# Batch norm over two DMA rings: hand-placed semaphores replaced by the framework's own dependencies

## The chip, the cores and the metric

One Trainium2 chip, one core. The metric is the device time of the slowest (here: the only) core in microseconds (us), lower is better. A kernel is compared with the kernel before in alternating rounds on one chip. A ratio is the mean time of one kernel's fast runs over that of the other's of the same rounds, so it is not quite the ratio of the medians quoted.

## The reference

```python
n, c, h, w = 32, 256, 128, 128          # x is float32, 537 MB; the output is as large
eps = 1e-5
return gamma * (x - mean) / np.sqrt(var + eps) + beta      # one scale and one shift per channel
```

The kernel turns this into `x * scale + shift` with 128 channels on the partitions: 64 tiles of 128 x 16384 float32 (8.389 MB, 64 KB per partition). Each tile is loaded, changed in place, and stored. There are three tile buffers.

## The kernel before

Loads are issued from the SP queue (one DMA ring), stores from the ACT queue (another ring). VectorE does columns 0 to 14336 of a tile in two pieces (the first of STEP = 2560 columns), ACT the rest. Every wait is written by hand inside a critical section.

```python
STEP = 2560; VCOLS = 14336; VLAST = 9216; NBUF = 3
# ... semaphores loaded[s], stored[s], vdone, adone, early, fetched, vec, act (cut)
with tc.tile_critical():
    # ... first half of tile 0, parameters, second half of tile 0 (cut)
    for i in range(1, NT):
        s, turn = i % NBUF, i // NBUF
        if turn:
            nc.sync.wait_ge(stored[s], 16 * turn)                  # store i-3 has left the buffer
        inst = nc.sync.dma_start(out=bufs[s][:], in_=xr[i]).then_inc(loaded[s], 16)
        if turn:
            inst._wait_ge(vdone, 2 * (i - 1) + 1)                  # first piece of tile i-1 is done
    # ... scale and shift (cut)
    vector_part(0, 0, HW // 2)._wait_ge(early, 16)
    vector_part(0, HW // 2, VCOLS)._wait_ge(*landed(0))
    for i in range(1, NT):
        vector_part(i, 0, STEP)._wait_ge(*landed(i))
        vector_part(i, STEP, VLAST if i == last else VCOLS)
    for i in range(last):
        nc.scalar.wait_ge(vdone, 2 * (i + 1))                      # both VectorE pieces of tile i
        inst = scalar_part(i, VCOLS)
        if i:
            inst._wait_ge(stored[(i - 1) % NBUF], 16 * ((i - 1) // NBUF + 1))   # store i-1 landed
        store(i)
    # ... last tile (cut)
```

So each ring is paced: load i+1 is held until load i has landed and its first piece is done; store i until store i-1 has landed and ACT has done its slice of tile i.

Of the kernel before, what the change touches and what calls it, by code (L numbers as in the profile page):

```python
# [8 lines left out]
NBUF = 3  # L9


STEP = 2560
VCOLS = 14336
VLAST = 9216


@with_exitstack
def kernel(
    ctx: ExitStack,
    tc: tile.TileContext,  # L20
    x: bass.AP,
    gamma: bass.AP,
    beta: bass.AP,
    running_mean: bass.AP,
    running_var: bass.AP,
    out: bass.AP,
):
    nc = tc.nc
    eps = 1e-5
    f32 = mybir.dt.float32  # L30

    N, C, H, W = x.shape
    P = nc.NUM_PARTITIONS
    assert C % P == 0
    NCB = C // P
    HW = H * W
    NT = N * NCB
    B = 32
    NQ = P // B
    NE = 16  # L40
    NPAR = 4

    xr = x.rearrange("n (cb p) h w -> (n cb) p (h w)", p=P)
    outr = out.rearrange("n (cb p) h w -> (n cb) p (h w)", p=P)

    params = ctx.enter_context(tc.tile_pool(name="params", bufs=1))
    data = ctx.enter_context(tc.tile_pool(name="data", bufs=1))
    bufs = [data.tile([P, HW], f32, name=f"t{s}", tag=f"t{s}") for s in range(NBUF)]
    rows = params.tile([B, NPAR * C], f32, name="rows", tag="rows")
    turned = params.tile([B, NPAR * C], f32, name="turned", tag="turned")  # L50
    par = params.tile([P, NPAR, NCB], f32, name="par", tag="par")
    eps_t = params.tile([P, 1], f32, name="eps_t", tag="eps")
    std_t = params.tile([P, NCB], f32, name="std_t", tag="std")
    rstd_t = params.tile([P, NCB], f32, name="rstd_t", tag="rstd")
    scale_t = params.tile([P, NCB], f32, name="scale_t", tag="scale")
    ms_t = params.tile([P, NCB], f32, name="ms_t", tag="ms")
    shift_t = params.tile([P, NCB], f32, name="shift_t", tag="shift")



    loaded = [tc.alloc_semaphore(f"loaded{s}") for s in range(NBUF)]
    stored = [tc.alloc_semaphore(f"stored{s}") for s in range(NBUF)]
    early = tc.alloc_semaphore("early")
    vdone = tc.alloc_semaphore("vdone")
    adone = tc.alloc_semaphore("adone")
    fetched = tc.alloc_semaphore("fetched")
    vec = tc.alloc_semaphore("vec")
    act = tc.alloc_semaphore("act")

    with tc.tile_critical():  # L70
        count = [0]

        def step(inst, sem=None, value=None):

            if sem is not None:
                inst._wait_ge(sem, value)
            elif count[0]:
                inst._wait_ge(vec, count[0])
            inst.then_inc(vec, 1)
            count[0] += 1  # L80
            return count[0]

        left, right = slice(0, HW // 2), slice(HW // 2, HW)
        last = NT - 1



        nc.sync.dma_start(out=bufs[0][:, left], in_=xr[0][:, left]).then_inc(early, 16)
        zeroed = step(nc.vector.memset(rows[:], 0.0))  # L89
        for r, ap in enumerate((running_var, gamma, beta, running_mean)):  # L90
            inst = nc.sync.dma_start(out=rows[0:NE, r * C : (r + 1) * C], in_=ap.partition_broadcast(NE))  # L91
            if r == 0:
                inst._wait_ge(vec, zeroed)
            inst.then_inc(fetched, 16)
        nc.sync.dma_start(out=bufs[0][:, right], in_=xr[0][:, right]).then_inc(loaded[0], 16)  # L95
        for i in range(1, NT):
            s, turn = i % NBUF, i // NBUF


            if turn:  # L100
                nc.sync.wait_ge(stored[s], 16 * turn)
            inst = nc.sync.dma_start(out=bufs[s][:], in_=xr[i]).then_inc(loaded[s], 16)
            if turn:
                inst._wait_ge(vdone, 2 * (i - 1) + 1)


        step(nc.vector.memset(eps_t[:], eps))  # L107
        step(nc.vector.transpose(out=turned[:], in_=rows[:]), fetched, 16 * NPAR)  # L108

        blocks = turned.rearrange("p (rc q b) -> p rc q b", q=NQ, b=B)  # L110
        flat = par.rearrange("p r cb -> p (r cb)")
        for q in range(NQ):
            placed = step(nc.vector.tensor_copy(out=flat[q * B : (q + 1) * B], in_=blocks[:, :, q, 0]))  # L113
        var_t, gamma_t, beta_t, mean_t = (par[:, r] for r in range(NPAR))
        nc.scalar.activation(  # L115
            out=std_t[:],
            in_=var_t,
            func=mybir.ActivationFunctionType.Sqrt,
            bias=eps_t[:],
            scale=1.0,  # L120
        )._wait_ge(vec, placed).then_inc(act, 1)
        step(nc.vector.reciprocal(out=rstd_t[:], in_=std_t[:]), act, 1)  # L122
        step(nc.vector.tensor_mul(out=scale_t[:], in0=gamma_t, in1=rstd_t[:]))  # L123
        step(nc.vector.tensor_mul(out=ms_t[:], in0=mean_t, in1=scale_t[:]))  # L124
        ready = step(nc.vector.tensor_sub(out=shift_t[:], in0=beta_t, in1=ms_t[:]))  # L125
        nc.vector.wait_ge(vec, ready)

        def vector_part(i, first, end):
            t, cb = bufs[i % NBUF], i % NCB
            return nc.vector.tensor_scalar(  # L130
                out=t[:, first:end],
                in0=t[:, first:end],
                scalar1=scale_t[:, cb : cb + 1],
                scalar2=shift_t[:, cb : cb + 1],
                op0=mybir.AluOpType.mult,
                op1=mybir.AluOpType.add,
            ).then_inc(vdone, 1)

        def scalar_part(i, first):
            t, cb = bufs[i % NBUF], i % NCB  # L140
            return nc.scalar.activation(  # L141
                out=t[:, first:],
                in_=t[:, first:],
                func=mybir.ActivationFunctionType.Identity,
                bias=shift_t[:, cb : cb + 1],
                scale=scale_t[:, cb : cb + 1],
            ).then_inc(adone, 1)

        def landed(i):
            return loaded[i % NBUF], 16 * (i // NBUF + 1)  # L150

        def store(i):
            s = i % NBUF
            nc.scalar.dma_start(out=outr[i], in_=bufs[s][:])._wait_ge(adone, i + 1).then_inc(stored[s], 16)

        vector_part(0, 0, HW // 2)._wait_ge(early, 16)
        vector_part(0, HW // 2, VCOLS)._wait_ge(*landed(0))
        for i in range(1, NT):
            vector_part(i, 0, STEP)._wait_ge(*landed(i))
            vector_part(i, STEP, VLAST if i == last else VCOLS)  # L160
        for i in range(last):
            nc.scalar.wait_ge(vdone, 2 * (i + 1))
            inst = scalar_part(i, VCOLS)
            if i:
                inst._wait_ge(stored[(i - 1) % NBUF], 16 * ((i - 1) // NBUF + 1))
            store(i)
        scalar_part(last, VLAST)._wait_ge(*landed(last))
        nc.scalar.wait_ge(vdone, 2 * NT)
        store(last)

        for s in range(NBUF):
            nc.sync.wait_ge(stored[s], 16 * ((NT - s + NBUF - 1) // NBUF))


# [28 lines left out]
```

## Time and profile before

| | before |
|---|---|
| median of 3 runs (range) | 2484.66 us (2484.28 to 2487.45) |
| VectorE / ACT busy | 508.8 us / 139.8 us |
| DMA | 9 in all 40 slices, 432 GB/s on the mean |
| period of one tile, both rings | 38.6 us |
| pause of the load ring, landing to next issue | 1.66 us |
| pause of the store ring, landing to next issue | about 2.1 us |

"Busy" is engine time. A DMA slice of 9 means that the 16 DMA engines were moving packets for 90% or more of that fortieth of the span. Issue to landing is the time from the instruction that issues a transfer to the semaphore that reports it complete. The lines behind the table stand in the prediction.

### The profile page before, as it was taken

What the parts mean: (1) busy time and instruction counts of PE and PEld (TensorE: products, weight loads), DVE (VectorE), ACT (ScalarE), POOL (GpSimd) and SP (SyncE); (2) the same over time, 40 slices, a digit from 0 to 9 for tenths busy, and PEclk for the clock granted to TensorE, in tenths of its full rate; (3) what the DMA queues carried; (4) which work ended last, traced back from release to release, by engine and by line L of the source; (5) the groups of instructions that cost most, each with busy time, mean ns of one, the idle gap of its engine ahead of it and who ended that gap; (6) DMA issues with size and microseconds to landing.
All of it is one profiled execution on the core that took longest, in us unless ns stands there. A gap on an engine that the chain in (4) does not pass through costs nothing.

```text
span 2483.3 us, 516 instructions
## 1 busy us (share of the span) xinstructions
DVE 508.8 (20%) x139; ACT 139.8 (6%) x66; POOL 0.2 (0%) x4
## 2 busy tenths in 40 slices
DVE  3122121221212212122121221212212122121220
ACT  0000000000000000000000000000000000000001
POOL 0000000000000000000000000000000000000000
DMA  9999999999999999999999999999999999999999
GB/s 415 430 439 434 428 436 436 435 433 430 432 433 438 430 432 433 435 424 437 437 428 436 438 436 429 437 435 430 436 437 436 430 437 435 429 437 435 433 433 408
DMA packets 18708, 1073.85 MB, mean 432 GB/s; under 512 B 2128, under 2 KB 2192, under 8 KB 2192
## 3 DMA queue, kind: packets, MB, share of 16 engines
q1 hardware_dynamic: 9488, 536.94, 50.1%
q10 hardware_dynamic: 9216, 536.88, 49.9%
q14 instruction: 4, 0.03, 0.0%
HBM read 536.94 MB, written 536.87 MB: 432 GB/s over the span
## 4 chain that ended last, share of the span: by engine, by line
DMA 93%; DVE 4%; another core or an unknown queue 1%; ACT 0%; issue 0%; SPq 0%; DVEq 0%
DMA t<-in_x_dram 93%; DVE t L130 4%; ACT t L141 0%; SPq L91 0%; DVE rows L89 0%; SPq L95 0%; DVE eps_t L107 0%; DVEq L198 0%; SPq L70 0%
## 5 line engine op out<-in xcount | busy, mean ns | idle before, releaser
L130 DVE TENSOR_SCALAR t<-t,scale_t,shift_t 128x11776 f32<-128x11776 f32 (+2 forms) x128 | 505.3, 3989 | 1930.4 <-DMA t<-in_x_dram 1930.2
L141 ACT ACTIVATE t<-t,shift_t,scale_t 128x2048 f32<-128x2048 f32 x64 | 138.2, 2159 | 2299.3 <-DMA out_dram<-t 2276.6
L108 DVE STREAM_TRANSPOSE turned<-rows 32x1024 f32<-32x1024 f32 x1 | 1.2, 1233 | 12.5 <-DMA rows<-in_running_mean_dram 12.5
L115 ACT ACT_TABLE_LOAD x1 | 1.3, 1283 | 0.9 <-SPq L70 0.9
L89 DVE MEMSET rows<- 32x1024 f32 x1 | 0.9, 912 | 1.2 <-SPq L70 1.2
L115 ACT ACTIVATE std_t<-par,eps_t 128x2 f32<-128x2 f32 x1 | 0.3, 296 | 14.7 <-DVE par L113 14.7
L113 DVE COPY par<-turned 32x8 f32<-32x8 f32 x4 | 0.6, 161 | 0.1
L122 DVE RECIPROCAL rstd_t<-std_t 128x2 f32<-128x2 f32 x1 | 0.2, 166 | 0.4 <-ACT std_t L115 0.4
L125 DVE TENSOR_TENSOR shift_t<-par,ms_t 128x2 f32<-128x2 f32 x1 | 0.2, 161 | 0.0
L124 DVE TENSOR_TENSOR ms_t<-par,scale_t 128x2 f32<-128x2 f32 x1 | 0.2, 161 | 0.0
L123 DVE TENSOR_TENSOR scale_t<-par,rstd_t 128x2 f32<-128x2 f32 x1 | 0.2, 160 | 0.0
L187 POOL MEMSET const-bfloat16-1.0<- 128x1 bf16 x1 | 0.1, 101 | 0.0
L187 POOL MEMSET const-uint8-127<- 128x1 uint8 x1 | 0.1, 101 | 0.0
L187 POOL MEMSET const-float32-0.0<- 128x1 f32 x1 | 0.1, 98 | 0.2 <-issue 0.2
L187 POOL MEMSET const-float32-1.0<- 128x1 f32 x1 | 0.1, 98 | 0.0
L107 DVE MEMSET eps_t<- 128x1 f32 x1 | 0.1, 59 | 0.1
## 6 DMA issues: line engine op xcount, KB each, us to landing
t<-in_x_dram SPq DMA_DIRECT2D x2, 4096.0 KB, 16.5
out_dram<-t ACTq DMA_DIRECT2D x64, 36.5
t<-in_x_dram SPq DMA_DIRECT2D x63, 37.0
rows<-in_running_var_dram SPq DMA_DIRECT2D x1, 16.0 KB, 11.3
rows<-in_gamma_dram SPq DMA_DIRECT2D x1, 16.0 KB, 11.1
rows<-in_beta_dram SPq DMA_DIRECT2D x1, 16.0 KB, 10.9
rows<-in_running_mean_dram SPq DMA_DIRECT2D x1, 16.0 KB, 11.3
```

The costliest lines, as they stand in the source:

```text
L89: zeroed = step(nc.vector.memset(rows[:], 0.0))
L107: step(nc.vector.memset(eps_t[:], eps))
L108: step(nc.vector.transpose(out=turned[:], in_=rows[:]), fetched, 16 * NPAR)
L113: placed = step(nc.vector.tensor_copy(out=flat[q * B : (q + 1) * B], in_=blocks[:, :, q, 0]))
L115: nc.scalar.activation(out=std_t[:], in_=var_t, func=mybir.ActivationFunctionType.Sqrt, bias=eps_t[:], scale=1.0,)._wait_ge(vec, placed).t ...
L122: step(nc.vector.reciprocal(out=rstd_t[:], in_=std_t[:]), act, 1)
L123: step(nc.vector.tensor_mul(out=scale_t[:], in0=gamma_t, in1=rstd_t[:]))
L124: step(nc.vector.tensor_mul(out=ms_t[:], in0=mean_t, in1=scale_t[:]))
L125: ready = step(nc.vector.tensor_sub(out=shift_t[:], in0=beta_t, in1=ms_t[:]))
L130: return nc.vector.tensor_scalar(out=t[:, first:end], in0=t[:, first:end], scalar1=scale_t[:, cb : cb + 1], scalar2=shift_t[:, cb : cb + 1 ...
L141: return nc.scalar.activation(out=t[:, first:], in_=t[:, first:], func=mybir.ActivationFunctionType.Identity, bias=shift_t[:, cb : cb + 1] ...
L187: nc = _bacc.Bacc("TRN2", target_bir_lowering=False, num_devices=1)
```

## The change

The intent is to keep the same order and pace of both rings, but let the framework (Tile) derive the waits from the accesses. Only two dependencies, those that pace the rings, are still named. The long diff, cut to its core:

```diff
-    bufs = [data.tile([P, HW], f32, name=f"t{s}", tag=f"t{s}") for s in range(NBUF)]
+    data = ctx.enter_context(tc.tile_pool(name="data", bufs=NBUF))
+    ctx.enter_context(tc.manual_schedule())
+    def after(inst, other):
+        info = mybir.DependencyInfo(mybir.DependencyClass.Sync, mybir.DependencyReason.DATA)
+        tc.add_manual_dep(inst.ins, other.ins.name, info, reason="pace of the rings")
+    def load(i):
+        t = data.tile([P, HW], f32, tag="t")
+        tiles[i] = t
+        return nc.sync.dma_start(out=t[:], in_=xr[i])
-    (twelve semaphores, the critical section, every wait_ge, _wait_ge and then_inc)
-    (three small tiles std_t, rstd_t, ms_t)
+    (one small tile tmp_t in their place)
+    for i in range(NT):
+        if i == 0:
+            vector_part(0, 0, HW // 2)
+            vector_part(0, HW // 2, VCOLS)
+        else:
+            firsts[i] = vector_part(i, 0, STEP)
+            vector_part(i, STEP, VLAST if i == last else VCOLS)
+        mine = scalar_part(i, VLAST if i == last else VCOLS)
+        if 0 < i < last:
+            after(mine, stores[i - 1])
+        stores[i] = nc.scalar.dma_start(out=outr[i], in_=tiles[i][:])
+        if 2 <= i and i + 1 < NT:
+            after(load(i + 1), firsts[i])
```

More of the change, by code (lines that the diff above doesn't have):

```diff
@@ L46 @@
     params = ctx.enter_context(tc.tile_pool(name="params", bufs=1))
-    data = ctx.enter_context(tc.tile_pool(name="data", bufs=1))
-    bufs = [data.tile([P, HW], f32, name=f"t{s}", tag=f"t{s}") for s in range(NBUF)]
-    rows = params.tile([B, NPAR * C], f32, name="rows", tag="rows")
-    turned = params.tile([B, NPAR * C], f32, name="turned", tag="turned")
-    par = params.tile([P, NPAR, NCB], f32, name="par", tag="par")
-    eps_t = params.tile([P, 1], f32, name="eps_t", tag="eps")
-    std_t = params.tile([P, NCB], f32, name="std_t", tag="std")
@@ L54 @@
-    rstd_t = params.tile([P, NCB], f32, name="rstd_t", tag="rstd")
-    scale_t = params.tile([P, NCB], f32, name="scale_t", tag="scale")
-    ms_t = params.tile([P, NCB], f32, name="ms_t", tag="ms")
-    shift_t = params.tile([P, NCB], f32, name="shift_t", tag="shift")
-    loaded = [tc.alloc_semaphore(f"loaded{s}") for s in range(NBUF)]
-    stored = [tc.alloc_semaphore(f"stored{s}") for s in range(NBUF)]
-    early = tc.alloc_semaphore("early")
-    vdone = tc.alloc_semaphore("vdone")
-    adone = tc.alloc_semaphore("adone")
@@ L66 @@
-    fetched = tc.alloc_semaphore("fetched")
-    vec = tc.alloc_semaphore("vec")
-    act = tc.alloc_semaphore("act")
-    with tc.tile_critical():
-        count = [0]
-        def step(inst, sem=None, value=None):
-            if sem is not None:
-                inst._wait_ge(sem, value)
-            elif count[0]:
-                inst._wait_ge(vec, count[0])
-            inst.then_inc(vec, 1)
-            count[0] += 1
-            return count[0]
-        left, right = slice(0, HW // 2), slice(HW // 2, HW)
-        last = NT - 1
-        nc.sync.dma_start(out=bufs[0][:, left], in_=xr[0][:, left]).then_inc(early, 16)
-        zeroed = step(nc.vector.memset(rows[:], 0.0))
-        for r, ap in enumerate((running_var, gamma, beta, running_mean)):
-            inst = nc.sync.dma_start(out=rows[0:NE, r * C : (r + 1) * C], in_=ap.partition_broadcast(NE))
-            if r == 0:
-                inst._wait_ge(vec, zeroed)
-            inst.then_inc(fetched, 16)
-        nc.sync.dma_start(out=bufs[0][:, right], in_=xr[0][:, right]).then_inc(loaded[0], 16)
-        for i in range(1, NT):
-            s, turn = i % NBUF, i // NBUF
-            if turn:
-                nc.sync.wait_ge(stored[s], 16 * turn)
-            inst = nc.sync.dma_start(out=bufs[s][:], in_=xr[i]).then_inc(loaded[s], 16)
-            if turn:
-                inst._wait_ge(vdone, 2 * (i - 1) + 1)
-        step(nc.vector.memset(eps_t[:], eps))
-        step(nc.vector.transpose(out=turned[:], in_=rows[:]), fetched, 16 * NPAR)
-        blocks = turned.rearrange("p (rc q b) -> p rc q b", q=NQ, b=B)
-        flat = par.rearrange("p r cb -> p (r cb)")
-        for q in range(NQ):
-            placed = step(nc.vector.tensor_copy(out=flat[q * B : (q + 1) * B], in_=blocks[:, :, q, 0]))
-        var_t, gamma_t, beta_t, mean_t = (par[:, r] for r in range(NPAR))
-        nc.scalar.activation(
-            out=std_t[:],
-            in_=var_t,
-            func=mybir.ActivationFunctionType.Sqrt,
-            bias=eps_t[:],
-            scale=1.0,
-        )._wait_ge(vec, placed).then_inc(act, 1)
-        step(nc.vector.reciprocal(out=rstd_t[:], in_=std_t[:]), act, 1)
-        step(nc.vector.tensor_mul(out=scale_t[:], in0=gamma_t, in1=rstd_t[:]))
-        step(nc.vector.tensor_mul(out=ms_t[:], in0=mean_t, in1=scale_t[:]))
-        ready = step(nc.vector.tensor_sub(out=shift_t[:], in0=beta_t, in1=ms_t[:]))
-        nc.vector.wait_ge(vec, ready)
-        def vector_part(i, first, end):
-            t, cb = bufs[i % NBUF], i % NCB
-            return nc.vector.tensor_scalar(
-                out=t[:, first:end],
-                in0=t[:, first:end],
-                scalar1=scale_t[:, cb : cb + 1],
-                scalar2=shift_t[:, cb : cb + 1],
-                op0=mybir.AluOpType.mult,
-                op1=mybir.AluOpType.add,
-            ).then_inc(vdone, 1)
-        def scalar_part(i, first):
-            t, cb = bufs[i % NBUF], i % NCB
-            return nc.scalar.activation(
-                out=t[:, first:],
-                in_=t[:, first:],
-                func=mybir.ActivationFunctionType.Identity,
-                bias=shift_t[:, cb : cb + 1],
-                scale=scale_t[:, cb : cb + 1],
-            ).then_inc(adone, 1)
-        def landed(i):
-            return loaded[i % NBUF], 16 * (i // NBUF + 1)
-        def store(i):
-            s = i % NBUF
-            nc.scalar.dma_start(out=outr[i], in_=bufs[s][:])._wait_ge(adone, i + 1).then_inc(stored[s], 16)
-        vector_part(0, 0, HW // 2)._wait_ge(early, 16)
-        vector_part(0, HW // 2, VCOLS)._wait_ge(*landed(0))
-        for i in range(1, NT):
-            vector_part(i, 0, STEP)._wait_ge(*landed(i))
-            vector_part(i, STEP, VLAST if i == last else VCOLS)
-        for i in range(last):
-            nc.scalar.wait_ge(vdone, 2 * (i + 1))
-            inst = scalar_part(i, VCOLS)
-            if i:
-                inst._wait_ge(stored[(i - 1) % NBUF], 16 * ((i - 1) // NBUF + 1))
-            store(i)
-        scalar_part(last, VLAST)._wait_ge(*landed(last))
-        nc.scalar.wait_ge(vdone, 2 * NT)
-        store(last)
-        for s in range(NBUF):
-            nc.sync.wait_ge(stored[s], 16 * ((NT - s + NBUF - 1) // NBUF))
@@ new lines @@
+    data = ctx.enter_context(tc.tile_pool(name="data", bufs=NBUF))
[3 more added lines that the diff above has]
+        tc.add_manual_dep(inst.ins, other.ins.name, info, reason="pace of the rings")
+    last = NT - 1
+    left, right = slice(0, HW // 2), slice(HW // 2, HW)
+    tiles, firsts, stores = {}, {}, {}
+    def load(i):
+        t = data.tile([P, HW], f32, tag="t")
+        tiles[i] = t
+        return nc.sync.dma_start(out=t[:], in_=xr[i])
@@ new lines @@
+    t = data.tile([P, HW], f32, tag="t")
+    tiles[0] = t
+    nc.sync.dma_start(out=t[:, left], in_=xr[0][:, left])
+    rows = params.tile([B, NPAR * C], f32, tag="rows")
+    nc.vector.memset(rows[:], 0.0)
+    for r, ap in enumerate((running_var, gamma, beta, running_mean)):
+        nc.sync.dma_start(out=rows[0:NE, r * C : (r + 1) * C], in_=ap.partition_broadcast(NE))
+    nc.sync.dma_start(out=t[:, right], in_=xr[0][:, right])
+    load(1)
+    load(2)
+    eps_t = params.tile([P, 1], f32, tag="eps")
@@ new lines @@
+    nc.vector.memset(eps_t[:], eps)
+    turned = params.tile([B, NPAR * C], f32, tag="turned")
+    nc.vector.transpose(out=turned[:], in_=rows[:])
+    par = params.tile([P, NPAR, NCB], f32, tag="par")
+    blocks = turned.rearrange("p (rc q b) -> p rc q b", q=NQ, b=B)
+    flat = par.rearrange("p r cb -> p (r cb)")
+    for q in range(NQ):
+        nc.vector.tensor_copy(out=flat[q * B : (q + 1) * B], in_=blocks[:, :, q, 0])
+    var_t, gamma_t, beta_t, mean_t = (par[:, r] for r in range(NPAR))
@@ new lines @@
+    scale_t = params.tile([P, NCB], f32, tag="scale")
+    shift_t = params.tile([P, NCB], f32, tag="shift")
+    tmp_t = params.tile([P, NCB], f32, tag="tmp")
+    nc.scalar.activation(
+        out=tmp_t[:],
+        in_=var_t,
+        func=mybir.ActivationFunctionType.Sqrt,
+        bias=eps_t[:],
+        scale=1.0,
+    )
+    nc.vector.reciprocal(out=tmp_t[:], in_=tmp_t[:])
+    nc.vector.tensor_mul(out=scale_t[:], in0=gamma_t, in1=tmp_t[:])
+    nc.vector.tensor_mul(out=tmp_t[:], in0=mean_t, in1=scale_t[:])
@@ new lines, with vector_part, scalar_part @@
+    nc.vector.tensor_sub(out=shift_t[:], in0=beta_t, in1=tmp_t[:])
+    def vector_part(i, first, end):
+        t, cb = tiles[i], i % NCB
+        return nc.vector.tensor_scalar(
+            out=t[:, first:end],
+            in0=t[:, first:end],
+            scalar1=scale_t[:, cb : cb + 1],
+            scalar2=shift_t[:, cb : cb + 1],
+            op0=mybir.AluOpType.mult,
+            op1=mybir.AluOpType.add,
+        )
+    def scalar_part(i, first):
+        t, cb = tiles[i], i % NCB
+        return nc.scalar.activation(
+            out=t[:, first:],
+            in_=t[:, first:],
+            func=mybir.ActivationFunctionType.Identity,
+            bias=shift_t[:, cb : cb + 1],
+            scale=scale_t[:, cb : cb + 1],
+        )
```

## The prediction

> **What bounds the kernel now.** I read the page first: the slices, the queues, the chain that ended last and the costliest groups. Then I read the waits of the engines and of the SP queue, the chain in order of time in the middle, and the busy table of the start, one middle period and the end.
>
> ```profile
> span 2483.3 us, 516 instructions
> DVE 508.8 (20%) x139; ACT 139.8 (6%) x66; POOL 0.2 (0%) x4
> DMA  9999999999999999999999999999999999999999
> DMA packets 18708, 1073.85 MB, mean 432 GB/s; under 512 B 2128, under 2 KB 2192, under 8 KB 2192
> q1 hardware_dynamic: 9488, 536.94, 50.1%
> q10 hardware_dynamic: 9216, 536.88, 49.9%
> ```
>
> The compute engines are busy for a fifth of the span or less; the DMA engines are above 90% in all 40 slices. Half of the bytes are loads on the SP ring, half are stores on the ACT ring. The bound is the transfer of 1073.85 MB, which no part of the change touches.
>
> ```profile
> 1017.55 1.62 DVE t L130
> 1019.17 0.02 issue
> 1019.19 36.97 DMA t<-in_x_dram
> 1056.15 0.03 issue
> 1056.18 1.62 DVE t L130
> 1057.80 0.02 issue
> ```
>
> This is the chain, in start and duration (us): a load takes 36.97 us to land, 0.03 us later VectorE does the 2560-column piece (1.62), and 0.02 us after it the next load is issued. One period is 1056.18 - 1017.55 = 38.63 us. The store ring has the same period: in the timeline ACTIVATE starts at 1003.04 and 1041.67, 38.63 apart, with 2.09 us of ACTIVATE, some 0.03 us to the issue, and 36.5 us to landing. Two tiles of 8.389 MB in 38.63 us are 434 GB/s.
>
> ```profile
> ACT t L141 <- DMA out_dram<-t: 2276.6, 62, 44.8
> SPq L101 <- DMA out_dram<-t: 1398.1, 61, 68.8
> SPq L102 <- DVE t L130: 985.0, 61, 16.2
> ```
>
> Here each row is engine, line, what it waited for, total us, times, longest. ACT's slice of a tile always waits for the store before it, not for VectorE. The SP queue first waits for the store that frees the buffer (about 23 us of a period), then for the 2560-column piece (985.0 / 61 = 16.1 us). So the pace is "one load and one store in flight", and the buffer comes free 16 us before it is wanted.
>
> ```profile
> 1005.50:1017.50 12.00, 0.00 (x0) 0.00 (x0) 0.00 (x0) 1.00 1.00 431
> 1019.30:1041.60 22.30, 6.18 (x1) 0.00 (x0) 0.00 (x0) 1.00 0.99 429
> 1041.70:1043.80 2.10, 0.00 (x0) 2.06 (x1) 0.00 (x0) 1.00 1.01 437
> 1056.20:1057.80 1.60, 1.60 (x2) 0.00 (x0) 0.00 (x0) 1.00 1.13 492
> ```
>
> The last two columns are DMA share and GB/s. In the 2.1 us in which no store is issued and in the 1.6 us in which no load is issued the engines stay full (437 and 492 GB/s), because the other ring has work. Windows of 2 us are coarse (others show 287 to 573), but the period's rate says the same. The gaps of the two rings cost nothing as long as they do not meet. Their middles stand about 14 us after and 24 us before each other.
>
> **What the Trainium skill says.** "DMA: Bandwidth & Descriptors", section "Where 436 GB/s comes from", gives 16 ports x 32 B x 850 MHz = 435.2 GB/s; the trace's 434 GB/s per period agrees. At that figure 1073.85 MB take an estimated 2467.5 us, 0.7% under the measured 2484.66. Faster by 2% would need a rate above it. The same page, "Queues, rings and completion order", says an engine goes round its queues packet by packet. The trace fits: leaving out the 2192 small packets, 16516 carry the data, 65 KB each; 65,536 B on 16 engines at 434 GB/s is a slot of 2.42 us, and 16 slots (8 load and 8 store packets per engine and tile) are 38.6 us, the period. So a pause of a ring shorter than about one slot should be filled by the other ring's packet (my inference). "Perfetto Trace Analysis", section "Identifying Dependency Chains", says that an instruction which waits for several engines may have extra wait instructions put before it; that is the one thing the generated waits could add. The trace of before gives its size: 0.02 to 0.05 us between an event and the issue it releases.
>
> **The change, part by part.**
>
> Removed: the critical section, 10 semaphores, the hand-placed waits. None shows as time: the first load is issued at 0.95 us, and no row names a barrier in mid-run. Nothing in bytes, tile shapes, column splits (2560, 14336, 9216) or engine assignment changes.
>
> Load i+1 before: store i-2 complete, and the first piece of tile i done. After: the slot of a three-slot tag is released by every reader of tile i-2, store last, and the added dependency names the same first piece. Same two conditions. The automatic form may also name ACT and VectorE for the old slot, both done long ago (16 us of slack). I allow two satisfied waits behind the last release: 2 x 0.04 = 0.08 us on the 1.66 us pause of the load ring. If it all fell on the path: 61 x 0.08 = 4.9 us. But the pause becomes 1.74, under a slot of 2.42, so it is filled: 0 to 1 us.
>
> Store i before: the ACT slice waits for both VectorE pieces and for store i-1, then the store is issued. After: the slice waits for the load and store i-1 (the pieces and the slice touch different columns, so no dependency between them is needed), and the store waits for slice and pieces. In steady state store i-1 ends last by 1041.67 - (1017.55 + 7.94) = 16.2 us, so the change of wait is worth 0.
>
> Tile 0: ACT waited 10.2 us for VectorE, started at 27.36 and the store went at 29.49. After, the slice can start when the right half has landed (about 23.85) and end at 25.94, beside VectorE, which ends at 27.33; the store goes at about 27.4, 2.1 us earlier. But in that stretch (16.0 to 29.5 us) the loads alone already moved 430 GB/s with DMA share 1.00. An earlier store takes its bytes from the loads: 0 us of end time. It should only set the rings about one slot apart from where they are now.
>
> Last tile: its slice has no store to wait for in either version (6.36 us beside 5.27 us of VectorE). If the automatic tracking did serialise them, the last store would go about 5.3 us later (2460 instead of 2454.7), while store 62 alone fills the engines: in 12.4 us at half rate it has moved some 2.7 MB of 8.39 when load 63 lands at 2448.3, and the remaining 5.7 MB need 13 us at 434 GB/s, so to 2461. Cost: 0 to 1 us.
>
> End: Tile's exit waits for its semaphores; up to a dozen satisfied waits at 0.04 us, 0.5 us. The scratch tiles merged into one change no wait: the five small VectorE operations (0.16 us each) and the square root run in order anyway, under the loads of tile 0.
>
> Sum: 2484.7 + 0 to 1 (load waits) + 0 (stores) + 0 (start) + 0.3 (exit) = about 2485.0.
>
> **The rivals.**
>
> First: the generated waits lengthen a ring's pause beyond the slot and the interlock slips. One ring then gains a slot of 2.4 us per tile, runs down the 16 us of slack in some 7 tiles, and has to wait for the other at every tile, so that pauses fall together. For: the store's 36.5 us to landing is hardly more than 15 slots (36.3), so its 2.1 us pause has little to spare. Against: loads of 38.05 and 37.66 us occur in the chain of before, and the rings went on as they were. If 0.7 us per tile idled it would make 2530; a full slot, 2630.
>
> Second: the dependency on the earlier store waits for its issue instead of its completion, so stores run unpaced, two in the ACT ring. ACT's idle time would be put down to loads. The bytes still bound it: 2475 to 2510, the upper part if loads are crowded out and the buffers come free late. Against: the added dependency is of the synchronising kind, whose natural meaning for a DMA is landing.
>
> Third: the earlier first store is a gain of its full 2.1 us, 2482.5. Against it speaks DMA share 1.00 in that stretch.
>
> **Range and chances.** The three runs of before spread over 2484.28 to 2487.45, so +-2 us is noise. The low end, 2480, is the third rival with luck; 2493 holds about 0.13 us of unhidden waits on each of 61 tiles. Faster by 2% (under 2435) is beyond the fabric figure: 0.01. Slower by 2% (over 2534) needs the first rival in its strong form: 0.04. The rest is same: 0.95.
>
> **What would show it.** Right: ACTIVATE still waits for the output DMA 61 or 62 times, for a total near 2280 us; the period is 38.6 us; load to landing 37.0 and store 36.5 us; DMA at 9 in all slices at 432 GB/s; ACT starts on tile 0 at about 24 us and the first store goes at about 27.4. Wrong: a period of 39 us or more, DMA slices of 8, the SP queue's wait moving from VectorE to the output DMA (first rival), ACT's idle put down to loads or to VectorE (second), or any barrier in mid-run. What would break the prediction is mainly a dependency that the automatic tracking adds by treating different columns of one tile as one, in a place where I found slack only for the order I assumed.

## The result, and the profile after

| | before | after |
|---|---|---|
| median of 6 runs (range) | 2485.11 us (2484.28 to 2487.45) | 2486.52 us (2484.09 to 2487.61) |
| ratio after / before | | 1.0002 (95%: 0.999 to 1.0015) |
| instructions in the profile | 516 | 758 |

The time is the same, inside the predicted range. The page after:

```profile
span 2484.2 us, 758 instructions
DVE 508.7 (20%) x139; ACT 139.8 (6%) x66; POOL 0.2 (0%) x4
DMA  9999999999999999999999999999999999999999
DMA packets 18709, 1073.86 MB, mean 432 GB/s; under 512 B 2128, under 2 KB 2192, under 8 KB 2192
```

Computation, bytes and rate have not moved; the 242 more instructions are waits: the trace has 388 separate wait instructions on ACT, VectorE and SP, where that of the kernel before has 136 (a few drains and branches fell away).

The waits of the engines after (who waited for whom; total us, times, longest us):

```profile
ACT t L117 <- DMA out_dram<-t: 2279.4, 62, 44.1
```

and the SP queue's own:

```profile
SPq L62 <- DVE t L106: 1953.7, 61, 67.2
SPq L62 <- DMA out_dram<-t: 411.1, 24, 17.3
```

ACT's slice still waits 62 times for the store before it, as predicted. The SP queue, which issues the loads, still waits 61 times for VectorE's first piece. Its total grew from 985 us because a generated wait instruction can name two semaphores at once (the store and VectorE) and is put down to the later one. The two rows together are 2365 us; the two rows of the kernel before were 1398.1 + 985.0 = 2383 us, so the queue waits no longer than it did.

The chain in the middle of the run after (start, duration, what; DVEq is VectorE's sequencer, here executing wait instructions):

```profile
981.18 36.86 DMA t<-in_x_dram
1018.05 0.03 issue
1018.07 0.02 DVEq L106
1018.10 0.05 issue
1018.14 0.05 DVEq L106
1018.19 0.05 issue
1018.24 1.62 DVE t L106
1019.87 0.02 SPq L62
1019.89 0.04 issue
1019.93 36.88 DMA t<-in_x_dram
```

From landing (1018.05) to the next issue (1019.93) it is 1.88 us in these rows, where before it was 1.66: two satisfied waits run on VectorE after the landing, one on SP after the piece. Of the 61 pauses 21 are like this one; 39 are about 1.81 us, which is the median. The load's median time to landing is 36.83 us instead of 36.97. Pause and landing together are 38.64 us in both kernels: the pause took from the landing what it gained.

The start, first before, then after (timeline; the last bracket is what ended the engine's idle time):

```profile
23.85 3.48 DVE L130 TENSOR_SCALAR t<-t,scale_t,shift_t 128x6144 f32<-128x6144 f32 x1 [1.27 <-DMA t<-in_x_dram]
27.36 2.09 ACT L141 ACTIVATE t<-t,shift_t,scale_t 128x2048 f32<-128x2048 f32 x1 [10.23 <-DVE t L130]
29.49 0.37 ACTq L154 DMA_DIRECT2D out_dram<-t  x1
```

```profile
23.28 3.48 DVE L106 TENSOR_SCALAR t<-t,scale_t,shift_t 128x6144 f32<-128x6144 f32 x1 [1.47 <-DMA t<-in_x_dram]
23.34 2.09 ACT L117 ACTIVATE t<-t,shift_t,scale_t 128x2048 f32<-128x2048 f32 x1 [6.90 <-DMA t<-in_x_dram]
26.84 0.37 ACTq L137 DMA_DIRECT2D out_dram<-t  x1
```

ACT now works beside VectorE on tile 0, and the first store goes 2.65 us earlier. From there on the rings stand differently: a store is issued 19.7 us after a load and the next load 19.0 us after that store (medians), where before it was 24.6 and 14.0. The timed runs show no effect of it.

### The profile page after: what moved, and what is told of

Same layout as the page of the kernel before. It is cut to its first block, busy times and chain, and to the rows that moved or that the text cites. A ratio compares the mean times of both kernels' runs of the same rounds, so it can differ in the third digit from the quotient of the medians.

```text
span 2484.2 us, 758 instructions
## 1 busy us (share of the span) xinstructions
DVE 508.7 (20%) x139; ACT 139.8 (6%) x66; POOL 0.2 (0%) x4
## 4 chain that ended last, share of the span: by engine, by line
DMA 91%; DVE 4%; another core or an unknown queue 2%; issue 0%; ACT 0%; DVEq 0%; SPq 0%
DMA t<-in_x_dram 91%; DVE t L106 4%; ACT t L117 0%; DVEq L106 0%; SPq L72 0%; SPq L62 0%; DVE rows L70 0%; DVE eps_t L79 0%
```

## The experiments

Theory: the bytes bound both kernels, and a ring's pause is filled by the other ring's packets, so the added waits and the shifted start cost nothing. Rivals: waits add to the period; or a longer pause lets the interlock of the rings slip; or pacing never mattered. Twelve kernels were run, each with 3 timed rounds and all of them correct.

"Packet records" below are the single DMA packets in a trace: start, duration, ring. I worked out from them how long the 16 engines stood idle, and by how much packets lasted longer than the usual 2.418 us.

### a1 and a2: more satisfied waits on VectorE, in the kernel before

```diff
         for i in range(1, NT):
+            for _ in range(6):            # a2: 24
+                nc.vector.wait_ge(*landed(i))
             vector_part(i, 0, STEP)._wait_ge(*landed(i))
```

(Two waits are fused into one instruction.)

> The kernel before with three more, already satisfied wait instructions on VectorE between a load's landing and the 2560-column piece, as the generated waits have them. My theory (the pause of the load ring is filled by a store packet as long as it is under a slot of 2.42 us): the pause from landing to the next issue grows from 1.66 to about 1.8 us, the load's issue to landing shrinks from 36.97 to about 36.83, the period stays 38.63 to 38.65, time 2485 +-2. Rival (the waits add to the period): 61 x 0.15 = +9 us, 2494. Third possibility: the added waits are what makes the period of the changed kernel 38.74 on the mean instead of 38.68, then it is 38.74 here too.

Measured: 2487.48 us, ratio 1.001 (0.9995 to 1.0025). In the chain 1.96 us from landing to issue (1017.94 to 1019.90) and 36.68 us to landing: together again 38.64.

> The same with 24 waits, fused by two into 12 instructions, some 0.5 us: pause about 2.2 us, still under a slot of 2.42. My theory: landing time shrinks by the same 0.5 us to about 36.4, time 2485 to 2488. Rival (adds up): +31 us, 2516. Rival (the interlock slips when the pause comes near the slot, and the pauses of the rings fall together): 2500 or more.

Measured: 2492.02 us (2489.11 to 2509.26), ratio 1.005 (1.0009 to 1.0091). The waits were dearer than expected, about 0.1 us each. The chain of a2:

```profile
981.54 35.80 DMA t<-in_x_dram
...
1018.54 1.62 DVE t L130
1020.18 35.77 DMA t<-in_x_dram
```

Landing at 1017.34, next issue at 1020.18: a pause of 2.84 us, and 35.80 us to landing. Again 38.64 in sum. The full addition (61 x 1.18 = 72 us) is refuted; what is left is 7 us by the medians. The expected 2485 to 2488 was a little low.

### a3, c1, c2, a4: a longer first piece, in the kernel before

```diff
-STEP = 2560
+STEP = 4608      # c1: 6144, c2: 7168, a4: 8192
```

> The kernel before with a first piece of 4608 columns: about 2.7 us from the two measured lengths (1.62 and 6.41 us), so a pause of about 2.75 us, above a slot of 2.42. Slip rival of the prediction: the load ring loses a slot of 2.4 us per tile, runs down its slack, and DMA idles: 2530 to 2630. Work-conserving theory: the store ring takes the extra slot, then has to wait for the load at some tiles (ACT's wait for the load appears), but a store is always in flight in the load's pause: 2485 to 2490.

Measured: 2490.14 us, ratio 1.0022 (1.0007 to 1.0037). The pause is 2.74 us, over one packet of 2.42, and nothing slipped: a store goes 23.5 us after a load from tile 2 to tile 60.

> First piece of 8192 columns, 4.55 us, pause 4.6 us, nearly two slots. Slip rival: at least as slow as with 4608 columns, over 2550. Work-conserving theory: still 2485 to 2495, with ACT waiting for loads or VectorE instead of the store at many tiles, and DMA at 9 in all slices.

Measured: 2680.98 us, ratio 1.0788 (1.0772 to 1.0804). The work-conserving theory (one ring always uses the time that the other leaves) is wrong here. From the waits of a4, and then one row of its busy table (the last two columns are DMA share and GB/s):

```profile
ACT t L141 <- DVE t L130: 2327.0, 59, 42.4
```

```profile
1053.90:1058.50 4.60, 4.56 (x2) 0.00 (x0) 0.00 (x0) 1.00 0.53 228
```

ACT now waits for VectorE at 59 tiles: the stores have caught up with the loads. From load issue to store issue the distance falls 24.1, 19.3, 14.4, ..., two packets per tile, and from tile 5 on stays at 5.58 us. In the load's pause the DMA share is 0.53: the store's last packets run out before the next load has its first. A window this short is coarse, because a packet counts where it starts (such windows of the kernel before read 0.60 to 1.32). The packet records are the better evidence: an engine stands idle for less than 0.01 us per tile in the kernel before and for 1.5 us in a4, nearly all of it between a load's landing and the next load's first packets. That is the difference between a filled and an unfilled pause.

> The kernel before with a first piece of 6144 columns: 3.5 us, pause of the load ring about 3.55 us, 1.9 more than now. In the packet records of the kernel before a load's first packet starts 3.8 us after its issue; where the engines stood idle (first piece of 8192 columns, no load pace) it starts after 0.96 us. So a load waits some 2.8 us for its turn, and that is the slack. Slack theory: the store is still issued 23 to 24 us after the load in every period, time 2485 to 2495. If the limit is one slot of 2.42 us on the pause, as predicted (already doubtful, since 4608 columns held): slip, over 2550.

Measured: 2582.82 us, ratio 1.0389 (1.0374 to 1.0405). The pause of 3.55 us slips; my slack of 2.8 us on top of 1.66 is refuted. The distance falls 21.0, 15.7, 10.7 and stays at 6.65.

> First piece of 7168 columns: 4.0 us, pause about 4.07, 2.4 more than now, at the edge of the slack of 2.4 (one packet) to 2.8 us. Open: either held as with 6144 columns (2485 to 2495) or slipping by two packets per tile as with 8192 (the distance from load issue to store issue falls by 4.8 us per tile to 5.0 us, time about 2670). It brackets the limit.

Measured: 2609.31 us, ratio 1.0489 (1.0467 to 1.051), distance 6.11 us. The limit therefore lies between a pause of 2.84 us (a2, held) and 3.55 us (c1, slipped).

### b1 and b2: one pacing dependency away, in the changed kernel

```diff
 # b1
-        if 0 < i < last:
-            after(mine, stores[i - 1])
 # b2
-            after(load(i + 1), firsts[i])
+            load(i + 1)
```

> The changed kernel without the dependency of ACT's slice on the store before it: two stores can be queued on the ACT ring. This is the second rival of the prediction by itself. If pacing of stores matters: 2500 or more, the SP queue's wait moving to stores. If only the bytes bound it: 2484 to 2490, ACT's idle put down to loads.

Measured: 2600.95 us, ratio 1.0476 (1.0452 to 1.05).

```profile
ACT t L117 <- DMA t<-in_x_dram: 2419.5, 64, 41.9
```

ACT's idle is put down to loads, as the second rival of the prediction had it, but the cost is more than four times its upper end (115 us, where 2510 would have been 25). The SP queue's wait did not move to stores, which I had expected of a slow result: it still waits 2416.5 us for VectorE and 60.9 us for stores. The stores catch up with the loads at once; the distance is 6.34 us.

> The changed kernel without the dependency of load i+1 on the first piece of tile i: a load goes as soon as its slot is free, so two loads can be queued and the load ring has no pause. If the pause matters: different from 2486 by over 10 us. If the bytes bound it: 2484 to 2490.

Measured: 2727.33 us, ratio 1.0973 (1.0953 to 1.0992). The waits of the engines, those of the SP queue, and two stretches of the busy table of b2:

```profile
ACT t L117 <- DMA out_dram<-t: 2521.5, 62, 44.2
```

```profile
SPq L62 <- DMA out_dram<-t: 2579.9, 61, 46.2
```

```profile
1013.50:1016.00 2.50, 2.46 (x2) 0.08 (x1) 0.00 (x0) 1.00 0.00 0
1056.00:1058.40 2.40, 2.35 (x2) 0.00 (x0) 0.00 (x0) 1.00 0.00 0
```

Both queues wait for the same event, the landing of a store: it frees the buffer for the next load and lets ACT go on. Load and store are then issued 2.0 us apart at every tile. In the stretches shown no packet starts at all (the last two columns are 0.00 and 0).

### b3 and b4: the two ends, in the changed kernel

```diff
 # b3: ACT's slice of tile 0 waits for both VectorE pieces, as before
+            held = vector_part(0, HW // 2, VCOLS)
+        if i == 0:
+            after(mine, held)
 # b4: the same for the last tile
+            second = vector_part(i, STEP, VLAST if i == last else VCOLS)
+        if i == last:
+            after(mine, second)
```

> The changed kernel with ACT's slice of tile 0 made to wait for both VectorE pieces, as in the kernel before. The first store goes at about 29 us instead of 26.84. My theory: time unchanged, 2486 +-2; the rings stand a slot nearer to the old phase. If the period of the changed kernel (38.74 on the mean against 38.68) comes from the phase and not from the waits, it goes back to 38.68 here and the time falls by 0 to 3 us. Third rival of the prediction: +2.1 us.

Measured: 2484.24 us, ratio 1.0001 (0.9986 to 1.0016). The first store goes at 29.17 us, the distances are back at 24.5 and 14.2. The time is the same to within 0.15% (3.7 us), which alone could not exclude the 2.1 us of the third rival. The packet records can: with the late first store an engine stands idle for 0.1 to 0.2 us in sum between 2 and 30 us (b3, before), so there was no gap that an earlier store could have filled. The period is 38.67 on the mean, with all the generated waits; the changed kernel's 38.74 was thus not the waits. a1, with added waits and the old phase, has 38.77, and b4, with the new phase, 38.76: the mean period varies by 0.1 us from run to run without order by waits or by phase, so 38.74 against 38.68 is no finding.

> The changed kernel with ACT's slice of the last tile made to wait for both VectorE pieces: the last store goes about 5.3 us later, at 2463.5. Predicted cost 0 to 1 us, because the store before it still fills the engines. If instead the end is set by the last store's issue and not by the bytes: +5.3 us.

Measured: 2488.45 us, ratio 1.001 (0.9994 to 1.0027): not told apart from nothing by the timed runs. The packet records show a hole: between 2460 and 2468 us the engines stand idle for 3.2 us in sum (per engine), where the changed kernel has none. The last store was issued at 2464.85, after the store before it had run dry. The prediction's 0 to 1 us was too little for the phase the rings have here.

### c3 and c4: a longer pause of the store ring, in the kernel before

```diff
             if i:
                 inst._wait_ge(stored[(i - 1) % NBUF], 16 * ((i - 1) // NBUF + 1))
+            for _ in range(72):
+                nc.scalar.wait_ge(adone, i + 1)
             store(i)
 # c4 has STEP = 8192 as well
```

> The kernel before with 72 satisfied waits (36 instructions, about 3 us) on ACT between the slice and the store: now the store ring's pause is over the slack, the load ring's is as before. Slack theory: the store ring loses packets, loads run ahead until they wait for the slot of store i-2, the pauses then fall together and the engines idle: 2600 or more, the SP queue's second wait gone. Rival (only a load's pause matters, because the chain of the end goes through loads): 2485 to 2495.

Measured: 2733.62 us, ratio 1.1011 (1.0974 to 1.1048). From the start of ACT's slice to the issue it is 4.88 or 5.18 us instead of 2.1. The SP queue's own waits and one stretch of the busy table of c3:

```profile
SPq L101 <- DMA out_dram<-t: 2590.7, 61, 69.3
SPq L102 <- DVE t L130: 19.8, 3, 8.9
```

```profile
1014.60:1019.40 4.80, 4.80 (x2) 0.00 (x0) 0.00 (x0) 1.00 0.51 218
```

The slip went the other way. The loads ran ahead until only the freed buffer held them (the wait for VectorE is gone, 3 times instead of 61). A store is now issued 4.9 us after a load, much as in b2. In the stretch shown no load is out: one has landed, and the next is issued at 1019.45, when the store has landed and its buffer is free. The store's last packets run out meanwhile, and the DMA share is 0.51. ACT's slice starts only at 1019.41, so that its waits then hold back the next store.

> Both pauses longer by about 3 us: first piece of 8192 columns and 72 satisfied waits on ACT. If the balance of the two pauses is what keeps the rings apart (each loses the same packet), the distance from load to store issue stays above 12 us and the time is 2485 to 2510, though each of the two alone costs 5% or more. If the length of a pause itself is what costs: 2680 or more, as with 8192 columns alone.

Measured: 2589.22 us, ratio 1.0417 (1.04 to 1.0434): neither expectation. The waits, of the engines and of the SP queue, are those of a paced kernel:

```profile
ACT t L141 <- DMA out_dram<-t: 2374.7, 62, 45.5
```

```profile
SPq L102 <- DVE t L130: 722.1, 61, 12.6
```

Balance did keep both rings free of each other's dependencies, and it is 92 us faster than the long piece alone. But the store is issued 33.1 us after the load, so the next load only 6.9 us after the store, and the time is 4% above the kernel before. So balance is not enough; whether it is this distance that costs the 4% is not shown.

### All kernels together

Worked out from the issue times and packet records of each profiled run. "Gaps" are the medians from load issue to store issue and from store issue to the next load (in c1 and c2 the second one alternates between about 33 and 36 us); "idle" is the mean engine's idle time after the first 30 us, counted over gaps of more than 0.03 us, with each packet put on the engine whose last packet ended where it starts; "long" is what packets over 2.6 us lasted beyond 2.418, per engine.

```
kernel             median us   gaps us      idle us   long us
b3_first_held       2484.24    24.5  14.2      0         2
before              2485.11    24.6  14.0      0         3
after               2486.52    19.7  19.0      0         4
a1_waits6           2487.48    24.3  14.3      0         5
b4_last_serial      2488.45    19.7  19.0      3         5
a3_step4608         2490.14    23.5  15.1      0         6
a2_waits24          2492.02    23.4  15.2      0         7
c1_step6144         2582.82     6.7  33.7     27        74
c4_both             2589.22    33.1   6.9     13        85
b1_no_store_pace    2600.95     6.3  34.4     31        85
c2_step7168         2609.31     6.1  34.8     45        80
a4_step8192         2680.98     5.6  36.5     87       114
b2_no_load_pace     2727.33     2.0  40.4    141        98
c3_act72            2733.62     4.9  37.6    136       113
```

In all kernels the bytes are the same. All seven whose smaller gap is 14 us or more are within 0.5% of the kernel before; all seven with a smaller gap under 7 us are 3.9 to 10.1% slower. No run lies between 7 and 14 us, and no run sets a gap by itself, so the table shows that gap and loss go together. Idle and long packets add up to the loss: in a4, 87 + 114 - 3 = 198 us, and the profiled spans differ by 2680.8 - 2483.3 = 197.5. This is bookkeeping, since all kernels move the same packets: it says where the time went, not why.

## Why the prediction was right

**The bound.** Right. In the kernel before the packets fill 2481 us per engine, practically all of the time from the first packet to the last; so too after. The waits are not on that path.

**The generated waits.** The mechanism was right, the size a bit larger: I allowed 0.08 us on the load ring's pause; it is 0.15 on the median (1.81 instead of 1.66), and 0.22 in the rows shown, where three wait instructions, not two, follow the last release, two of them on VectorE. They were filled as expected: pause and landing sum up to 38.6 us in the kernel before and with up to 1.18 us added (a1, a2). b3, with all generated waits, runs at 2484.24. Why a2 and a3 are 0.2 to 0.5% slower is not settled; their long packets (6 to 7 us instead of 3) are about half of it.

**Slot and threshold.** This step was right in kind and wrong in its number, and it would have misled with a larger change. I compared the pause with one packet of 2.42 us. But a ring is silent for longer than its pause: in the packet records of the kernel before, a load's last packet ends 2.8 us before its landing is seen, and a new transfer whose engines stand idle shows its first packet 0.96 us after issue (b2). The 2.8 us is no fixed cost: in the kernels before and after, an engine nearly always moves one packet of the other ring (2.42 us) between a transfer's last data packet and the 4-byte packet that comes just before the landing. Where no such packet comes between, as for the stores of b2 and c1, it is 0.36 us. What fills the silence is also more than one packet: between two loads an engine moves 4 to 6 store packets in a row in the kernel before, and in a2 mostly 6 or 7, of the 8 that a tile has. Where this ends I can't work out; the runs give a bracket. With both rings paced and the store ring's pause as before, load pauses of 2.74 and 2.84 us held (a3, a2), those of 3.55 us and more slipped (c1, c2, a4). So the change used up about 0.15 us of a margin of 1.2 to 1.9 us.

**Stores and the two ends.** Right for the steady state and for tile 0: the first store went at 26.84 (predicted 27.4), and neither the timed runs nor the packet records (b3) show a gain from it. Its shift of the rings was undersized: two slots (from 24.6 to 19.7 us) where I had one. Right that the last tile is not serialised; its possible cost was understated: b4 leaves the engines idle for 3.2 us, where I had 0 to 1. (A slip of counting without effect: the semaphores removed are twelve, not ten.)

**The rivals.** The first, the slip, is real, and its upper end was undersized: 2583 to 2734 us in c1, c2, a4 and c3, where I had 2530 for part of a slot and 2630 for a full one; in a4 it ran at two slots per tile, not one. The change stays clear of it. The second would have made 2601 (b1), not 2475 to 2510: I had reasoned that the bytes bound any order, and b1 and b2 refute that. The third, a gain of 2.1 us at the start, is too small for the timed runs; the packet records of the start (b3) speak against it.

**What stays open.** By the table some 40 to 85% of the loss in the slow kernels is in packets that last up to 4.0 to 4.5 us instead of 2.4. In c1, a4 and b1 they sit in the first and about the fourth eighth of a load, in c4 also in the first of a store. By their places they come where a ring, their own or the other, starts again after silence. I have no run that separates their cause, and so can't say why c4, with hardly any idle time, still loses 4%.

## What to carry to other kernels

Letting the framework derive the waits was safe here, where the bound is elsewhere and the waits fall in a pause that another stream fills: 242 more instructions changed the time by 0.02% (95%: -0.1 to +0.15%). Not safe to drop are the dependencies that no data needs: the two that pace the rings are worth 5 and 10%. Where two DMA streams share engines, look at the distance between their issues as well as at the DMA share, and ask what each stream would wait for if it ran a little faster; if that is the other's end, their pauses can meet, as they did in b2 and c3.

## What the Trainium skill lacked or had wrong

- "DMA: Bandwidth & Descriptors", section "Issuing engines are not separate DMA queues", says that DMAs initiated on several engines interleave and that doing so only saves issue time. It lacks that the interleaving can fail to fill the pauses of two paced rings: the same transfers took 2484 to 2492 us with issues 14 us or more apart and 2583 to 2734 us with issues under 7 us apart.
- The same page, "Latency and other measured facts", gives about 600 ns to the first byte for this kind of DMA. The records show 0.96 us from issue to the first packet on idle engines (b2). From a transfer's last data packet to its reported landing they show 0.36 us, or 2.8 us where a packet of the other ring comes between; the section has no figure for this part on this path. It also gives no duration for a packet of 64 KB; one lasts 2.418 us here, and up to 4.5 us in the slow kernels (c4).
- "Perfetto Trace Analysis", section "Identifying Dependency Chains", mentions the extra wait instructions but gives no cost of one that is already satisfied: 0.07 us on VectorE here (pauses of 1.88 against 1.81 us), about 0.1 us each in a row of twelve (a2).
